# A planned matmul order: one 512-column matmul behind each narrow one, and new engine costs in the plan

## The chip, the core and the metric

The kernel runs on one core of one Trainium2 chip. The metric is the device time of one execution in microseconds; lower is better. A core has five engines with a queue of instructions each: TensorE (PE in the profile, with its weight loads as PEld), VectorE (DVE), ScalarE (ACT), GpSimd (POOL) and SyncE (SP). An engine takes its own instructions in order, and semaphores hold one engine for another. TensorE multiplies a stationary operand (the weights, loaded by LDWEIGHTS) with a moving one whose columns stream through, and writes to PSUM.

## What is computed

One layer of a trunk with 512 tokens and a width of 2048, in float32. A normalised input is projected to three branches (q, k, v and a gate, four heads of 128 each), to forget-gate logits and to three merge gates:

```python
hn = rmsnorm(x, norm_g)
proj = jnp.einsum('bsd,dc->bsc', hn, w_in)
...
gates = jax.nn.sigmoid(proj[..., QKVG_COLS + N_HEADS:] + b_gate).reshape(b, s, N_BRANCH, D_MODEL)
...
ya = forgetting_attention(qa, ka, to_heads(br[:, :, 0, 2]), f_logit)      # softmax with a decay bias
yb = chunked_relpos_attention(qb, kb, to_heads(br[:, :, 1, 2]), rel_bias)  # chunks with a relative bias
yc = stick_breaking_attention(...)                                         # causal, in log space
ys = ys * jax.nn.silu(br[:, :, :, 3])
up = jnp.einsum('bsnw,nwd->bsnd', ys, w_up)
merged = jnp.sum(gates * up, axis=2)
return x + jnp.einsum('bsd,de->bse', merged, w_out)
```

## The kernel before

**Products in parts.** A float32 matrix product is made of three single-pass products: each operand is split into a rounded high part (fp32r) and the rest, and high x high, low x high and high x low are added up in PSUM. The moving operand of the big products is a weight tile and always 512 columns wide, the stationary one a 128 x 128 block of the activations (`mm`, L264, whose instruction is L265). ScalarE makes the high part of a weight tile (`prep`, L366) and VectorE the low part (L371); two or three tiles are prepared ahead. Most of the input projection and the whole output projection go by a seven-product (Strassen) scheme, whose combinations of weights are added by a DMA that accumulates (`add_up`, issued by GpSimd at L281) and by VectorE (L574).

**Small work of the heads.** Twelve heads (four for each of the branches C, B, A) are handled beside the big products. For each head q, k and the gate are turned by TensorE, four 128-column transposes each (`turned`, L796, instruction L801). Scores are made by `mm3` (L258, instructions L260 to L262): for the query block i three matmuls of 128 x (i + 1) columns, so 128, 256, 384 and 512, with a further 128-column one for the mask in branch A (L898). The softmax or stick-breaking weights are turned again by `soft_trans` (L916, instruction L926; 4, 3, 2 and 1 transposes), and multiplied with the values by `av` (L1002, instructions L1014 to L1016; 512, 384, 256 and 128 columns). Later the merged outputs are turned by `turned_m` (L1275, instruction L1282), 64 transposes in four runs of 16, and `merged_b` (L1308) makes from them the parts that the output projection needs.

**What sets the order.** The order on TensorE, VectorE and ScalarE is fixed when the program is built, by a planner (`Flow`, L65) that imitates the three engines. Every piece of work is a Python generator that yields what it needs: an event, a number of buffers, or an engine with a cost. `run` (L125) takes, again and again, the offered step that can start first by the planned clocks, and among equal ones that with the earliest due time (its ready time plus the `slack` of its task); then it advances that engine's planned clock by the cost and issues the instructions. The main stream of big products (`stream`, L1412) is a task with a slack of 1e9, so that it gives way to all others and fills what they leave. Most tasks of the heads have 5, those of the last head 0.3 (its gate, values and SiLU 4). The costs come from three functions (L151 to L160):

```python
def mm_us(n, x=1):
    return x * max(0.115, n / 2400 + 0.0133)
def act_us(n, x=1):
    return x * (0.075 + 0.00095 * n)
def dve_us(n, x=1):
    return x * (0.1 + 0.00105 * n)
```

A group of narrow matmuls is one step: four transposes are offered as one step of 0.11 x 4, the three matmuls of `mm3` and `av` as one each. The transfers are imitated as well: `fetch` (L276, a load by SyncE) and `add_up` move on a planned line of transfers, `line`, and return an event with a landing time. These times decide only where an instruction is put in its queue; on the chip the semaphores decide when it starts.

Of the kernel before, what the change touches and what calls it, by code (L numbers as in the profile page):

```python
# [64 lines left out]
class Flow:  # L65
# [7 lines left out]
    def __init__(self):  # L73
        self.clock = [0.0] * 3
        self.idle = [0.0] * 3
        self.now = self.fin = 0.0
        self.tasks = []

    def set(self, event):
        event.t = self.fin  # L80
# [4 lines left out]
    def spawn(self, gen, slack, ready=None):  # L85
        task = Task(gen, slack, self.now if ready is None else ready)
        self.tasks.append(task)
        self.advance(task)

    def advance(self, task):  # L90
# [34 lines left out]
    def run(self):  # L125
        while self.tasks:
            best = None
            for t in list(self.tasks):
                if t.engine is None:
                    self.advance(t)  # L130
            for t in self.tasks:
                if t.engine is not None:
                    key = (max(self.clock[t.engine], t.ready), t.due)
                    if best is None or key < best[0]:
                        best = key, t
            assert best is not None, [
                (t.gen.__qualname__.split(".")[-1], t.gen.gi_frame.f_lineno,
                 (len(t.wait[0].free), t.wait[1]) if isinstance(t.wait, tuple) else "event") for t in self.tasks]
            (start, _), t = best
            e = t.engine  # L140
            self.idle[e] += start - self.clock[e]
            self.now = start
            self.clock[e] = start + t.cost
            t.ready = self.clock[e]
            self.fin = t.fin = self.clock[e] + self.LATE[e]
            t.prev = e
            t.engine = t.wait = None
            self.advance(t)


def mm_us(n, x=1):  # L151
    return x * max(0.115, n / 2400 + 0.0133)


def act_us(n, x=1):
    return x * (0.075 + 0.00095 * n)


def dve_us(n, x=1):
    return x * (0.1 + 0.00105 * n)  # L160


@with_exitstack
def hybrid_kernel(
# [50 lines left out]
    def blk(i):  # L215
        return slice(i * P, (i + 1) * P)
# [38 lines left out]

        nc.vector.scalar_tensor_tensor(to, a, -1.0, b, op0=ALU.mult, op1=ALU.subtract)

    def mm3(ps, lh, ll, rh, rl, start, stop, more=False):  # L258

        nc.tensor.matmul(ps, lh, rh, start=start, stop=False, skip_group_check=more)  # L260
        nc.tensor.matmul(ps, lh, rl, start=False, stop=False, skip_group_check=more)  # L261
        nc.tensor.matmul(ps, ll, rh, start=False, stop=stop, skip_group_check=more)  # L262

    def mm(ps, w, x, start=False, stop=False, more=False):  # L264
        nc.tensor.matmul(ps, w, x, start=start, stop=stop, skip_group_check=more)  # L265
# [13 lines left out]

    def add_up(to, src, ready, kb):  # L280
        nc.gpsimd.dma_start(to, src, accum_op=ALU.add)  # L281
        line[1] = max(line[1], ready + 1.0) + kb / 170.0
        return Event(line[1] + 2.5)

    def stored(slots, n, kb):

# [88 lines left out]
    def products(u, ps, kts, tbs, block, first=False, last=False, bank=None, done=None, outer=False):  # L375

        for group in [[tb] for tb in tbs] if outer else [tbs]:
            if bank is not None:
                for tb in group:
                    yield bank[0], 1  # L380
                    ps[tb] = bank[1]()
            for j, kt in enumerate(kts):
                for tb in group:
                    yield lambda: block(kt, tb) is not None
                    h, lo, ev = block(kt, tb)
                    yield ev
                    yield PE, mm_us(S, 2)
                    mm(ps[tb], h, u.hi[:, j, :], first and j == 0)
                    mm(ps[tb], lo, u.hi[:, j, :])
            yield u.ready  # L390
            for j, kt in enumerate(kts):
                for tb in group:
                    yield PE, mm_us(S)
                    mm(ps[tb], block(kt, tb)[0], u.lo[:, j, :], stop=last and j == len(kts) - 1)
            if last:
                for tb in group:
                    spawn(done(tb), 1.0, flow.fin)
# [347 lines left out]
    class Head:  # L745
# [49 lines left out]

        def turned(self, r):  # L796

            yield PE, 0.11 * QB
            ps = att()
            for tb in range(QB):  # L800
                nc.tensor.transpose(ps[:, blk(tb)], self.c[tb][:, blk(r)], identf)  # L801
            self.taken()
            return ps
# [81 lines left out]
        def soft_scores(self, i):  # L885
            n = self.n
            m = (i + 1) * P
            for e in (("p", Q), ("p", K), ("b",)):
                yield self.event(*e)
            yield atts, 1  # L890
            (qh, ql), (kh, kl) = self.t[Q], self.t[K]
            yield PE, mm_us(m, 3) + (mm_us(P) if n == A else 0)
            ps = att()[:, :m]
            mm3(ps, qh[:, blk(i)], ql[:, blk(i)], kh[:, :m], kl[:, :m], True, n == B)
            p = self.p[i]
            mx, sm = small("mx"), small("sm")
            if n == A:
                nc.tensor.matmul(ps[:, blk(i)], identb, mska, start=False, stop=True)  # L898
# [12 lines left out]
            nc.vector.reciprocal(sm, sm)  # L911
            yield ACT, act_us(m) + 0.1
            nc.scalar.activation(p, p, AF.Copy, scale=sm)
            set_(self.event("s", i))

        def soft_trans(self, j):  # L916
            for i in range(QB):
                yield self.event("s", i)
            if j:
                yield self.event("a", j - 1)  # L920
            yield from self.parts_of(j)
            yield atts, 1
            yield PE, 0.11 * (QB - j)
            ps = att()
            for i in range(j, QB):
                nc.tensor.transpose(ps[:, blk(i)], self.p[i][:, blk(j)], identf)  # L926
# [16 lines left out]
        def stick_scores(self, i):  # L943
# [5 lines left out]
            yield PE, mm_us(m, 3)  # L949
            ps = att()[:, :m]  # L950
            mm3(ps, qh[:, blk(i)], ql[:, blk(i)], kh[:, :m], kl[:, :m], True, True)
            if self.nth("s", QB):
                give(t2s, 4)
            z = self.p[i]
# [47 lines left out]
        def av(self, j):  # L1002
# [3 lines left out]
                yield self.event("o", j - 1)  # L1006
            else:
                yield atts, 1
            yield PE, mm_us(S - j * P, 3)
# [4 lines left out]
            nc.tensor.matmul(o, vh[:, blk(j)], h, start=j == 0, stop=False)  # L1014
            nc.tensor.matmul(o, vl[:, blk(j)], h, start=False, stop=False)  # L1015
            nc.tensor.matmul(o, vh[:, blk(j)], lo, start=False, stop=j == QB - 1)  # L1016
            set_(self.event("o", j))
            give(t2s, (2, 0, 2, 4)[j])
# [58 lines left out]
    def quad(parts, g, done, early=False):  # L1077
# [8 lines left out]
        def mms(kts):  # L1086
            def go(u):
# [9 lines left out]
                else:  # L1097
# [3 lines left out]
                    for part in range(3):  # L1101
                        if part == 2:
                            yield u.ready
                        for j, kt in enumerate(kts):
                            yield (raw_hi[kt], raw_ev[kt], raw_ev[kt])[part]
                            yield PE, mm_us(S, QB)
                            w = u.lo if part == 2 else u.hi
                            for tb in tbs:
                                mm(ps[tb], block(kt, tb)[part == 1], w[:, j, :], kt + part == 0)
                if early and (kts[-1] + 1) % 4 == 0:  # L1110
                    four = range(kts[-1] - 3, kts[-1] + 1)
# [91 lines left out]
    def split_y(i):  # L1203
        def go():
# [3 lines left out]
            if (n, h) == (A, NH - 1):  # L1208
                yield last_head.event("y")
                t = last_head.y  # L1210
            else:
                yield t2s, 1
                t = t2("yr")
                yield fetch(t, yd[n, h], flow.now, 256)
# [60 lines left out]
    def turned_m(g, i):  # L1275
        for tb in range(QB):
            yield merged_ev[NB - 1, g, tb]
        yield atts, 1
        yield PE, 0.11 * QB
        ps = att()  # L1280
        for tb in range(QB):
            nc.tensor.transpose(ps[:, blk(tb)], merged[g, tb][:, blk(i)], identf)  # L1282
        turns[g] = turns.get(g, 0) + 1
        if turns[g] == QB:
# [207 lines left out]
```

## Time and profile before

| | before |
|---|---|
| median of 3 runs | 1319.29 us (1318.65 to 1319.43) |
| the profiled execution | 1319.42 us |
| its span, first to last instruction | 1317.7 us |
| TensorE busy, matmuls | 1307.4 us, 6034 |
| VectorE busy | 1023.4 us (78%) |
| ScalarE busy | 752.4 us (57%) |
| GpSimd busy | 91.5 us (7%) |
| moved by DMA | 266.03 MB |
| granted TensorE clock | 1.00 |

A row of the timeline gives the start in us from the span's start, the duration, the engine, the line, the operation, the tiles (out<-in), the shape and how many instructions were merged into the row; in brackets stands idle time ahead of it with what ended it. A row of a group has the count after the x, then the busy time and the mean duration in ns, then idle time of the engine just ahead of the group. Matmuls overlap: the next one starts while the last is still draining, so the share of busy time and the mean duration don't say what one costs; the distance from start to start does. In a row of waits stand the engine and line that waited, what released it, the total in us, the number of times and the longest.

### The profile page before, as it was taken

To read this page: it belongs to the slowest core of one execution; us is meant where nothing else is said; L and a number is where in the kernel's file an instruction comes from. 1 tells how busy PE (TensorE), PEld (TensorE's weight loads), DVE (VectorE), ACT (ScalarE), POOL (GpSimd) and SP (SyncE) were. 2 spreads that over 40 slices of the span, in tenths; PEclk is the share of its full clock that TensorE was granted. 3 is DMA by queue.
4 is the path that set the end of the run, shared out by engine and by line. 5 is a ranking of instruction groups with operands and counts; after the bars stand their busy time and mean duration, and the time that the engine had idled before them with its cause. 6 is when DMAs were issued, how large, how long until landed. Compare 5 with 4: busy or idle time off the path is not lost.

```text
span 1317.7 us, 17190 instructions
## 1 busy us (share of the span) xinstructions
PE 1307.4 (99%) x6034; PEld 1078.6 (82%) x6034; DVE 1023.4 (78%) x1420; ACT 752.4 (57%) x1271; POOL 91.5 (7%) x115
## 2 busy tenths in 40 slices
PE   9999999999999999999999999999999999999998
PEld 7788888888888888888888888888887788878787
DVE  6877787887878777687776877778789668798667
ACT  7655464564557646566466664667558545454342
POOL 0000001110011101111011110111000000000110
PEclk9999999999999999999999999999999999999999
DMA  9745677866777757777577775777786656637883
GB/s 361 233 121 145 181 210 191 235 170 180 211 192 229 201 164 232 175 228 203 170 225 176 225 207 168 224 177 217 225 250 196 236 192 205 164 95 250 246 240 128
DMA packets 89063, 266.03 MB, mean 202 GB/s; under 512 B 11264, under 2 KB 11264, under 8 KB 88976
## 3 DMA queue, kind: packets, MB, share of 16 engines
q1 hardware_dynamic: 71552, 206.16, 46.1%
q0 software_dynamic: 14976, 54.53, 23.2%
q10 hardware_dynamic: 2448, 4.24, 0.8%
q8 instruction: 47, 0.77, 0.2%
q14 instruction: 40, 0.33, 0.1%
HBM read 245.19 MB, written 19.70 MB: 201 GB/s over the span
## 4 chain that ended last, share of the span: by engine, by line
PE 95%; DMA 2%; ACT 1%; DVE 1%; issue 0%; POOL 0%; ACTq 0%; POOLq 0%; DVEq 0%
PE acc L265 87%; DMA raw<-in_w_out 2%; PE att L801 1%; PE att L926 1%; PE att L260 1%; PE att L261 1%; PE att L262 1%; DMA raw<-in_w_col 1%; PE att L1016 1%; PE att L1015 1%; PE att L1282 1%; ACT wh L366 1%; PE att L265 1%; PE att L1014 0%; DMA sg<-gl 0%; DVE wl L371 0%
## 5 line engine op out<-in xcount | busy, mean ns | idle before, releaser
L371 DVE TENSOR_TENSOR wl<-raw,wh 128x1024 fp32r<-128x1024 f32 (+1 forms) x405 | 493.4, 1220 | 209.5 <-PE acc L265 122.7
L366 ACT ACTIVATE wh<-raw 128x1024 fp32r<-128x1024 f32 (+1 forms) x405 | 426.7, 1055 | 369.5 <-PE acc L265 283.2
L265 PE MATMUL acc<-wh,x 128*128 128x512 f32 x1664 | 429.5, 392 | 0.0
L265 PEld LDWEIGHTS acc<-wh,x 128*128 128x128 f32 x1664 | 308.8, 188 | 65.7 <-ACT xn L476 1.7
L265 PE MATMUL acc<-wh,t 128*128 128x512 f32 x1056 | 272.7, 391 | 0.0
L265 PE MATMUL acc<-wl,x 128*128 128x512 f32 x832 | 230.1, 390 | 0.0
L265 PEld LDWEIGHTS acc<-wh,t 128*128 128x128 f32 x1056 | 196.7, 188 | 40.3
L265 PEld LDWEIGHTS acc<-wl,x 128*128 128x128 f32 x832 | 155.8, 188 | 33.0 <-DVE wl L371 0.4
L265 PE MATMUL acc<-wl,t 128*128 128x512 f32 x528 | 149.3, 390 | 0.0
L281 POOL DMA_DIRECT2D raw<-in_w_col x88 | 76.3, 867 | 878.1 <-DMA raw<-in_w_col 198.2
L574 DVE TENSOR_TENSOR raw<-raw,raw 128x1024 f32<-128x1024 f32 x104 | 126.7, 1218 | 0.0
L265 PEld LDWEIGHTS acc<-wl,t 128*128 128x128 f32 x528 | 98.4, 188 | 19.6
L265 PE MATMUL acc<-wh,m 128*128 128x512 f32 x416 | 105.2, 390 | 1.5 <-ACT wh L366 1.4
L265 PE MATMUL acc<-wh,y 128*128 128x512 f32 x384 | 103.7, 390 | 1.3 <-DVE sg L1248 1.3
L265 PEld LDWEIGHTS acc<-wh,m 128*128 128x128 f32 x416 | 77.9, 188 | 18.5 <-ACT wh L366 2.3
L265 PEld LDWEIGHTS acc<-wh,y 128*128 128x128 f32 x384 | 71.7, 188 | 16.8 <-DVE sg L1248 2.2
L265 PE MATMUL acc<-wl,y 128*128 128x512 f32 x192 | 59.7, 391 | 0.0
L265 PE MATMUL acc<-wl,m 128*128 128x512 f32 x208 | 58.1, 390 | 0.1
L246 ACT ACTIVATE ah<-att 128x512 fp32r<-128x512 f32 (+3 forms) x48 | 21.0, 438 | 48.1 <-PE att L926 48.1
L265 PEld LDWEIGHTS acc<-wl,m 128*128 128x128 f32 x208 | 38.9, 188 | 8.5 <-DVE wl L371 0.5
L250 DVE TENSOR_TENSOR al<-att,ah 128x512 fp32r<-128x512 f32 (+3 forms) x48 | 23.5, 490 | 25.5 <-ACT ah L246 24.8
L265 PEld LDWEIGHTS acc<-wl,y 128*128 128x128 f32 x192 | 35.7, 188 | 7.3
(179 smaller groups left out, 1115.9 us busy)
## 6 DMA issues: line engine op xcount, KB each, us to landing
raw<-in_w_col SPq DMA_DIRECT2D x235, 512.0 KB, 5.0
raw<-in_w_col POOLq DMA_DIRECT2D x88, 512.0 KB, 8.0
raw<-in_w_out SPq DMA_DIRECT2D x40, 512.0 KB, 3.6
raw<-in_w_up SPq DMA_DIRECT2D x24, 512.0 KB, 3.6
sg<-gl SPq DMA_DIRECT2D x48, 256.0 KB, 5.0
raw<-in_w_out POOLq DMA_DIRECT2D x16, 512.0 KB, 5.9
gl<-u SPq DMA_DIRECT2D x22, 256.0 KB, 9.2
gl<-s SPq DMA_DIRECT2D x22, 256.0 KB, 4.6
```

The costliest lines, as they stand in the source:

```text
L246: nc.scalar.activation(hi, src, AF.Copy)
L250: nc.vector.tensor_sub(lo, src, f(hi))
L260: nc.tensor.matmul(ps, lh, rh, start=start, stop=False, skip_group_check=more)
L261: nc.tensor.matmul(ps, lh, rl, start=False, stop=False, skip_group_check=more)
L262: nc.tensor.matmul(ps, ll, rh, start=False, stop=stop, skip_group_check=more)
L265: nc.tensor.matmul(ps, w, x, start=start, stop=stop, skip_group_check=more)
L281: nc.gpsimd.dma_start(to, src, accum_op=ALU.add)
L366: nc.scalar.activation(u.hi, u.raw, AF.Copy)
L371: nc.vector.tensor_sub(u.lo, u.raw, f(u.hi))
L574: nc.vector.tensor_add(to.raw, to.raw, self.raw)
L801: nc.tensor.transpose(ps[:, blk(tb)], self.c[tb][:, blk(r)], identf)
L926: nc.tensor.transpose(ps[:, blk(i)], self.p[i][:, blk(j)], identf)
```

## The change

Four things are changed.

1. `run` remembers whether TensorE's last step was a narrow one (a cost under 0.2, so up to 384 columns) of another task than the main stream. If so, and if the main stream offers a matmul that is ready at that time, all other TensorE steps are passed over, except those of tasks with a slack below 1.
2. The groups of matmuls are offered one at a time: the transposes (a cost of `TURN` each), `mm3`, `av`, and the pairs and fours in the main stream.
3. The costs: no lower bound of 0.115 for a matmul, 0.05 for a transpose, and higher fixed parts for VectorE and ScalarE. The planned landing of an accumulating transfer is the later of its source's landing and the line's time, plus 6.5, and the line is advanced less.
4. `split_y`, which loads a stored branch output again, first waits in the plan for the event that it was written.

```diff
+        self.main = None
+        self.narrow = False
...
+        if slack > 1e8:
+            self.main = task
...
+            main = self.main
+            full = (self.narrow and main is not None and main.engine == PE
+                    and main.ready <= self.clock[PE] + 0.02)
             for t in self.tasks:
+                if full and t.engine == PE and t is not main and t.slack >= 1:
+                    continue
...
+            if e == PE:
+                self.narrow = t is not self.main and t.cost < 0.2
...
-def mm_us(n, x=1):
-    return x * max(0.115, n / 2400 + 0.0133)
+def mm_us(n):
+    return n / 2400 + 0.0133
+
+
+TURN = 0.05
...
-    return x * (0.075 + 0.00095 * n)
+    return x * (0.13 + 0.0009 * n)
...
-    return x * (0.1 + 0.00105 * n)
+    return x * (0.15 + 0.00105 * n)
...
-        nc.tensor.matmul(ps, lh, rh, start=start, stop=False, skip_group_check=more)
-        nc.tensor.matmul(ps, lh, rl, start=False, stop=False, skip_group_check=more)
-        nc.tensor.matmul(ps, ll, rh, start=False, stop=stop, skip_group_check=more)
+        nc.tensor.matmul(ps, lh, rh, start=start, stop=False)
+        yield PE, mm_us(m)
+        nc.tensor.matmul(ps, lh, rl, start=False, stop=False)
+        yield PE, mm_us(m)
+        nc.tensor.matmul(ps, ll, rh, start=False, stop=stop)
...
-        line[1] = max(line[1], ready + 1.0) + kb / 170.0
-        return Event(line[1] + 2.5)
+        line[1] += kb / 250.0
+        return Event(max(line[1], ready) + 6.5)
...
-            yield PE, 0.11 * QB
+            yield PE, TURN
             ps = att()
             for tb in range(QB):
+                if tb:
+                    yield PE, TURN
                 nc.tensor.transpose(ps[:, blk(tb)], self.c[tb][:, blk(r)], identf)
...
             else:
+                yield heads[i].event("y")
                 yield t2s, 1
```

`soft_trans` and `turned_m` are changed as `turned` is; `av` yields ahead of each of its three matmuls, and the main stream ahead of each of its own. No matmul is added or taken away.

More of the change, by code (lines that the diff above doesn't have):

```diff
@@ L256, in minus, with mm3 @@
         nc.vector.scalar_tensor_tensor(to, a, -1.0, b, op0=ALU.mult, op1=ALU.subtract)
[L258 to L262, printed above, removed]
+    def mm3(ps, lh, ll, rh, rl, start, stop, m):
+        nc.tensor.matmul(ps, lh, rh, start=start, stop=False)
[3 more added lines that the diff above has]
+        nc.tensor.matmul(ps, ll, rh, start=False, stop=stop)
     def mm(ps, w, x, start=False, stop=False, more=False):
@@ L386, in products @@
                     yield ev
-                    yield PE, mm_us(S, 2)
+                    yield PE, mm_us(S)
                     mm(ps[tb], h, u.hi[:, j, :], first and j == 0)
+                    yield PE, mm_us(S)
                     mm(ps[tb], lo, u.hi[:, j, :])
@@ L891, in soft_scores @@
             (qh, ql), (kh, kl) = self.t[Q], self.t[K]
-            yield PE, mm_us(m, 3) + (mm_us(P) if n == A else 0)
+            yield PE, mm_us(m)
             ps = att()[:, :m]
-            mm3(ps, qh[:, blk(i)], ql[:, blk(i)], kh[:, :m], kl[:, :m], True, n == B)
+            yield from mm3(ps, qh[:, blk(i)], ql[:, blk(i)], kh[:, :m], kl[:, :m], True, n == B, m)
             p = self.p[i]
@@ L897, in soft_scores @@
             if n == A:
+                yield PE, mm_us(P)
                 nc.tensor.matmul(ps[:, blk(i)], identb, mska, start=False, stop=True)
@@ L922, in soft_trans @@
             yield atts, 1
-            yield PE, 0.11 * (QB - j)
+            yield PE, TURN
             ps = att()
             for i in range(j, QB):
+                if i > j:
+                    yield PE, TURN
                 nc.tensor.transpose(ps[:, blk(i)], self.p[i][:, blk(j)], identf)
@@ L948, in stick_scores @@
             (qh, ql), (kh, kl) = self.t[Q], self.t[K]
-            yield PE, mm_us(m, 3)
+            yield PE, mm_us(m)
             ps = att()[:, :m]
-            mm3(ps, qh[:, blk(i)], ql[:, blk(i)], kh[:, :m], kl[:, :m], True, True)
+            yield from mm3(ps, qh[:, blk(i)], ql[:, blk(i)], kh[:, :m], kl[:, :m], True, True, m)
             if self.nth("s", QB):
@@ L1008, in av @@
                 yield atts, 1
-            yield PE, mm_us(S - j * P, 3)
+            n = mm_us(S - j * P)
+            yield PE, n
             if j == 0:
@@ L1014, in av @@
             nc.tensor.matmul(o, vh[:, blk(j)], h, start=j == 0, stop=False)
+            yield PE, n
             nc.tensor.matmul(o, vl[:, blk(j)], h, start=False, stop=False)
+            yield PE, n
             nc.tensor.matmul(o, vh[:, blk(j)], lo, start=False, stop=j == QB - 1)
@@ L1105, in go @@
                             yield (raw_hi[kt], raw_ev[kt], raw_ev[kt])[part]
-                            yield PE, mm_us(S, QB)
                             w = u.lo if part == 2 else u.hi
                             for tb in tbs:
+                                yield PE, mm_us(S)
                                 mm(ps[tb], block(kt, tb)[part == 1], w[:, j, :], kt + part == 0)
@@ L1278, in turned_m @@
         yield atts, 1
-        yield PE, 0.11 * QB
+        yield PE, TURN
         ps = att()
         for tb in range(QB):
+            if tb:
+                yield PE, TURN
             nc.tensor.transpose(ps[:, blk(tb)], merged[g, tb][:, blk(i)], identf)
```

## The prediction

> **What bounds the kernel now.** I began with the page: the span, the busy shares and the chain that ended last.
>
> ```profile
> span 1317.7 us, 17190 instructions
> PE 1307.4 (99%) x6034; PEld 1078.6 (82%) x6034; DVE 1023.4 (78%) x1420; ACT 752.4 (57%) x1271; POOL 91.5 (7%) x115
> PE 95%; DMA 2%; ACT 1%; DVE 1%; issue 0%; POOL 0%; ACTq 0%; POOLq 0%; DVEq 0%
> ```
>
> TensorE is busy for 99% of the span and is 95% of the chain. A better order on VectorE or ScalarE can therefore gain only what TensorE still waits for. The view of waits, for TensorE alone, shows how much that is:
>
> ```profile
> PE att L417 <- DVE identb L310: 1.9, 1, 1.9
> PE acc L265 <- ACT wh L366: 1.4, 1, 1.4
> PE acc L265 <- DVE sg L1248: 1.3, 1, 1.3
> PE att L265 <- DVE wl L371: 1.1, 1, 1.1
> PE att L801 <- ACT w L793: 0.4, 1, 0.4
> ```
>
> The first wait is the start-up, ahead of the planned order. The other four, 1.4 + 1.3 + 1.1 + 0.4 = 4.2 us, are all that a better order could win, 0.3% of the span. Everything else is the sum of what TensorE's instructions cost in the place where they stand, so the question is what a narrow matmul costs behind a narrow one and what it costs between two wide ones. The mean durations of the groups don't say this, because matmuls overlap. The distance from start to start in the timeline does. First the wide ones, undisturbed:
>
> ```profile
> 1294.51 1.98 PE L265 MATMUL acc<-wh,m 128*128 128x512 f32 x8
> 1296.33 1.07 PE L265 MATMUL acc<-wl,m 128*128 128x512 f32 x4
> 1297.23 1.98 PE L265 MATMUL acc<-wh,m 128*128 128x512 f32 x8
> ```
>
> Twelve matmuls start in 1297.23 - 1294.51 = 2.72 us, which is 0.227 us each.
>
> **A narrow matmul among narrow ones.** Sixteen transposes in a row, with wide ones around them:
>
> ```profile
> 1053.54 1.08 PE L265 MATMUL acc<-wh,y 128*128 128x512 f32 x4
> 1054.46 1.91 PE L1282 MATMUL att<-identf,sg 128*128 128x128 f32 x16
> 1056.12 0.70 PE L265 MATMUL acc<-wl,y 128*128 128x512 f32 x2
> 1056.66 1.09 PE L265 MATMUL acc<-wh,y 128*128 128x512 f32 x4
> ```
>
> From 1053.54 to 1056.66 are 3.12 us. Six wide matmuls take 6 x 0.227 = 1.36, and 1.76 are left for sixteen transposes: 0.110 us each.
>
> **A narrow matmul between wider ones.** The order of before has one kind of place where a transpose stands alone, the last of each head's `soft_trans`. A wide matmul is ahead of it and a 256-column one behind:
>
> ```profile
> 217.86 1.08 PE L265 MATMUL acc<-wh,t 128*128 128x512 f32 x4
> 218.78 0.27 PE L926 MATMUL att<-identf,p 128*128 128x128 f32 x1
> 218.81 0.36 PE L1014 MATMUL att<-ah,vh 128*128 128x256 f32 x1
> 219.01 0.28 PE L1015 MATMUL att<-ah,vl 128*128 128x256 f32 x1
> 219.13 0.28 PE L1016 MATMUL att<-al,vh 128*128 128x256 f32 x1
> 219.25 0.63 PE L265 MATMUL acc<-wl,t 128*128 128x512 f32 x2
> ```
>
> From 217.86 to 219.25 are 1.39 us. Four wide ones take 0.91. The 256-column ones take 0.12 each (219.01 to 219.13 to 219.25), so three take 0.36. That leaves 0.12 us for the lone transpose. It is not cheaper than in a run. The start shown behind it comes 0.03 us later, but the next one comes 0.20 later where 0.12 is usual: the matmul behind it has begun and stands. I read this as its weights not being there. A load fits under a wide matmul, but the load of the matmul *behind* a narrow one has only the narrow one to lie under.
>
> The same with 128-column score matmuls (`mm3`):
>
> ```profile
> 171.44 1.07 PE L265 MATMUL acc<-wh,x 128*128 128x512 f32 x4
> 172.34 0.22 PE L260 MATMUL att<-qkh,qkh 128*128 128x128 f32 x1
> 172.40 0.28 PE L261 MATMUL att<-qkl,qkh 128*128 128x128 f32 x1
> 172.51 0.27 PE L262 MATMUL att<-qkh,qkl 128*128 128x128 f32 x1
> 172.63 1.13 PE L265 MATMUL acc<-wh,x 128*128 128x512 f32 x4
> 173.60 1.07 PE L265 MATMUL acc<-wl,x 128*128 128x512 f32 x4
> ```
>
> From 171.44 to 173.60 are 2.16 us. Eight wide ones take 1.81, three narrow ones 0.35, or 0.115 each. After the first, whose weights came in under a wide matmul, only 0.06 passes (172.34 to 172.40): that is the streaming of 128 columns. The shortfall comes back at the end, where four wide ones take 173.60 - 172.63 = 0.97 and not 0.91. So each matmul costs the longer of two times, its own streaming (0.227, 0.12, 0.06) and the load behind it (about 0.11). Such a sum doesn't depend on the order.
>
> The Trainium skill, TensorE: Matmul & The Clock Gate, section LDWEIGHTS (loading the stationary operand), gives a load as its columns over 1.2 GHz, by estimate 107 ns for 128 columns, whatever stands ahead; this speaks against the change, and the rows agree. The same page, section Back-to-back issue gap, has an isolated 128-column matmul at 128/2.4 + 2.5, by estimate 56 ns; where that governed, a narrow one between wide ones would cost half of what the lone transpose above shows.
>
> **The change, part by part.** *The rule in `run`.* After a narrow matmul that isn't the main stream's, the next one must be the main stream's if that is ready, except for tasks of slack below 1 (the last head's scores, transposes and `qk`). `turned`, `soft_trans`, `turned_m`, `mm3` and `av` now offer their matmuls one by one, so that the rule reaches them. The transposes:
>
> ```profile
> L926 PE MATMUL att<-identf,p 128*128 128x128 f32 x120 | 20.8, 271 | 0.0
> L801 PE MATMUL att<-identf,v 128*128 128x128 f32 x66 | 12.8, 274 | 0.0
> L801 PE MATMUL att<-identf,w 128*128 128x128 f32 x66 | 12.8, 273 | 0.4 <-ACT w L793 0.4
> L1282 PE MATMUL att<-identf,sg 128*128 128x128 f32 x64 | 7.6, 272 | 0.0
> L801 PE MATMUL att<-identf,c 128*128 128x128 f32 x12 | 1.8, 272 | 0.0
> ```
>
> They are 328: 22 for each of twelve heads (three turns of 4, and 4 + 3 + 2 + 1) and 64 in `turned_m`. The places where one follows another directly are 15 in a head and 60 in the four runs of 16, 240 in all. The last head keeps 12 of its 15, which leaves 228 to be split. What one split costs is the difference between the lone transpose and one in a run, 0.12 - 0.11 = 0.01 us, with both ends read from rows of two decimals: between 0 and 0.02. The sum is 228 x 0.01 = +2.3 us, with bounds of 0 and +4.6. I take the middle, since the rows themselves stand there. A split below zero is excluded by the lone one's 0.12, unless a 512-column matmul behind differs from a 256-column one; that is the first rival.
>
> The 128-column scores and `av` products cost 0.115 in a run, and the sum of longer times gives the same when each has a wide one behind it: 0. The 256- and 384-column ones stream for longer (0.12 and more) than a load takes and hide it already: 0.
>
> *The transposes come later.* A run of four is now spread over three more wide matmuls, 3 x 0.227 = 0.7 us, and sixteen over fifteen, 3.4 us. TensorE does main work meanwhile; what comes later is ScalarE's and VectorE's work on the result. Costed at nothing: attention keeps a whole head of distance from its consumer, and ScalarE prepares weights well ahead:
>
> ```profile
> ACT wh L366 <- PE acc L265: 283.2, 178, 5.7
> ```
>
> In 178 places ScalarE had already waited for TensorE to release a weight buffer, 283.2/178 = 1.6 us on average. That is the cover; a jam longer than this reaches TensorE.
>
> *The costs.* VectorE's and ScalarE's become more exact: for 1024 columns the plan had 0.1 + 0.00105 x 1024 = 1.175 us and now has 1.225, and for 512 on ScalarE it had 0.561 and now has 0.591.
>
> ```profile
> L371 DVE TENSOR_TENSOR wl<-raw,wh 128x1024 fp32r<-128x1024 f32 (+1 forms) x405 | 493.4, 1220 | 209.5 <-PE acc L265 122.7
> L643 ACT ACTIVATE u<-acc 128x512 f32<-128x512 f32 x26 | 15.5, 597 | 11.4 <-PE acc L265 11.3
> ```
>
> Measured are 1.220 and 0.597. TensorE's become less exact: a transpose is planned at 0.05 (it was 0.11), a 128-column matmul at 0.067 (it was 0.115), so in a head the plan runs ahead of TensorE by about 22 x 0.06 = 1.3 us. No queue is re-ordered by hand; the queues of VectorE and ScalarE follow the plan, and a queue that has an early consumer of a TensorE result holds up the weight conversions behind it. Together I put both at -0.5 us, one of the smaller waits gone, with ends of -4.2 (all of them gone) and about +4 (their like again).
>
> *`add_up`.* The accumulating transfer now lands in the plan at its source's landing or the queue's time, whichever is later, plus 6.5 us:
>
> ```profile
> raw<-in_w_col POOLq DMA_DIRECT2D x88, 512.0 KB, 8.0
> ```
>
> Measured is 8.0. Before, with the queue free, it was also 1.0 + 512/170 + 2.5 = 6.5, but it pushed back every later transfer in the plan. Which transfer is issued when hangs on freed buffers, so nothing moves on the queues of SyncE and GpSimd but by the plan's new times. Zero, with the ends in the previous item. The wait for a stored branch output in `split_y` is long fulfilled by then: zero.
>
> **Sum.** The profiled execution took 1319.42 us, beside a median of 1319.29. With +2.3 - 0.5 = +1.8 it would be 1321.2, and against the median 1321.1; I say 1321.1, which is 0.14% up. About 0.2% (2.6 us) is what a measurement of this kernel can tell from no change, so the forecast is "the same, on the slow side".
>
> **Rivals.** *A narrow matmul between 512-column ones costs its streaming alone, 0.06.* It would need the load of the wide one's weights to start before the narrow one does. About 310 transposes would gain 0.05 and some 66 score and output products 0.055: 15.5 + 3.6 = 19 us, so 1300. Against it stand the lone transpose and the last `mm3` product above, both already with something wider behind. By the 56 ns of the Trainium skill (TensorE: Matmul & The Clock Gate, section Back-to-back issue gap) the 310 transposes alone would gain an estimated 17 us. Chance 0.05.
>
> *The waits go.* With true costs most of the 4.2 us fall away and the splits cost nearly nothing: about 1319.3 - 3.5 = 1316. For it: all four are waits for VectorE or ScalarE. Against it: the wait for `wh` (1.4) is behind a weight transfer, which no cost mends. Chance 0.15.
>
> *Slower: late transposes jam VectorE ahead of the weights.* The place is the start of the output projection, where the last sixteen transposes feed `merged_b`, whose VectorE and ScalarE work stands in one queue with the weight splits of L371.
>
> ```profile
> 1157.51 1.91 PE L1282 MATMUL att<-identf,sg 128*128 128x128 f32 x16
> 1186.12 5.44 PE att L265 x24
> ```
>
> The first row is the timeline's, the second the chain's, where the matmuls that use these parts begin. In between TensorE waits 1.1 us for L371 as it is. If the splits of the merged parts come 3.4 us later, L371 waits behind more of them, and the wait grows towards 1.1 + 3.4; with the splits' 2.3 the kernel is at about 1325. It decides if the cover at L371 there is under those 3.4 us, which a wait of 1.1 suggests; against it, 27 us lie between the transposes and their use, and the plan sees the lateness. Together with the upper half of the splits' bounds: chance 0.33.
>
> *The rule changes little*, since main isn't ready in the plan when it asks: then 1319. This is inside "same".
>
> **How the numbers follow.** The forecast's case (same) has 0.47, slower 0.33, faster 0.15 + 0.05 = 0.20. The range goes from 1316, the centre of the waits' rival, to 1325, the jam's time: about 0.12 is left below and 0.07 above. "Same" alone would be 1316.7 to 1321.9.
>
> **What would show it.** The transposes' groups should keep their counts, and in the timeline each should stand alone between L265 rows. From wide to wide across one the distance should be 0.227 + 0.12. If it is 0.28, the first rival holds. The four waits of TensorE, in particular that for L371 near 1174 us, tell the other two apart. The prediction is wrong if TensorE's waits change by more than 2 us or if a lone transpose costs under 0.10 or over 0.14 us.

## The result, and the profile after

The changed kernel takes 1324.21 us (median of 5 runs, 1324.16 to 1328.08) where the kernel before takes 1319.29: the ratio is 1.0044, 95% interval 1.003 to 1.0058. It is slower by about 5 us. "The same, on the slow side" was wrong; the time lies inside the range, near its upper end.

The page of the changed kernel, of an execution of 1328.08 us:

```profile
span 1326.4 us, 17218 instructions
PE 1313.2 (99%) x6034; PEld 1074.5 (81%) x6034; DVE 1018.5 (77%) x1420; ACT 751.5 (57%) x1271; POOL 91.5 (7%) x115
```

The matmul count is that of before, and VectorE and ScalarE do no more. TensorE is still busy for 99%. This execution is the longest of the five. TensorE's clock was down to half in places in it, which explains a part of that (seven matmuls at 0.2 us too much, 1.4 us) and which the experiments come back to; a second profile of the same kernel, of an execution of 1325.42 us, lies beside the experiments.

The transposes in the timeline, TensorE's rows near 953 us (lines are from the changed file: L281 is the big product, L948 `soft_trans`):

```profile
952.62 0.62 PE L281 MATMUL acc<-wh,x 128*128 128x512 f32 x2
953.07 0.39 PE L281 MATMUL acc<-wl,x 128*128 128x512 f32 x1
953.30 0.27 PE L948 MATMUL att<-identf,p 128*128 128x128 f32 x1
953.33 0.48 PE L281 MATMUL acc<-wl,x 128*128 128x512 f32 x1
953.65 0.27 PE L948 MATMUL att<-identf,p 128*128 128x128 f32 x1
953.68 0.49 PE L281 MATMUL acc<-wh,x 128*128 128x512 f32 x1
954.00 0.27 PE L948 MATMUL att<-identf,p 128*128 128x128 f32 x1
954.03 0.48 PE L281 MATMUL acc<-wh,x 128*128 128x512 f32 x1
954.35 0.27 PE L948 MATMUL att<-identf,p 128*128 128x128 f32 x1
954.38 0.71 PE L281 MATMUL acc<-wh,x 128*128 128x512 f32 x2
954.92 0.62 PE L281 MATMUL acc<-wl,x 128*128 128x512 f32 x2
```

The rule does what it says. From 952.62 to 954.92 are 2.30 us with eight wide matmuls (8 x 0.227 = 1.816) and four transposes, which leaves 0.484, or 0.121 us for each; over the twelve heads a lone transpose takes 0.117 on average. In a run of sixteen they took 0.110. A 512-column matmul behind a narrow one hides nothing: its start is shown 0.03 us after the transpose's, and then it takes 0.32 until the next one starts.

TensorE's waits after:

```profile
PE acc L281 <- DVE sg L1274: 4.4, 3, 2.3
PE att L434 <- DVE identb L326: 1.9, 1, 1.9
PE acc L281 <- ACT wh L382: 1.7, 2, 1.4
PE att L281 <- DVE wl L387: 0.3, 1, 0.3
PE att L281 <- ACT wh L382: 0.3, 1, 0.3
PE acc L281 <- DVE wl L387: 0.2, 1, 0.2
PE att L1041 <- DVE al L264: 0.2, 1, 0.2
```

Without the start-up they were 4.2 us and are 7.1. The wait for the merge gates (`sg`) has grown from 1.3 to 4.4, and the one for the low parts at the output projection has shrunk from 1.1 to 0.3. The first of these is at the end of the last head. ScalarE's row and TensorE's rows there:

```profile
1030.08 1.28 ACT L1258 ACT_TABLE_LOAD   x1
1032.79 1.19 PE L281 MATMUL acc<-wh,y 128*128 128x512 f32 x4 [1.58 <-DVE sg L1274]
1038.08 1.50 PE L281 MATMUL acc<-wh,y 128*128 128x512 f32 x4 [2.26 <-DVE sg L1274]
1039.37 1.05 PE L281 MATMUL acc<-wl,y 128*128 128x512 f32 x2
1040.22 1.91 PE L281 MATMUL acc<-wh,y 128*128 128x512 f32 x4
```

The sigmoids of the merge gates come after the last head's last exponential, with a table load ahead of them (1030.08). They let the up projection's banks go, so TensorE stops until they are through. Before, the table load stood here:

```profile
1024.66 1.28 ACT L1232 ACT_TABLE_LOAD   x1
```

Counted in the traces, the main stream had by then started 4113 wide matmuls; in the changed kernel it had started 4128 and had no bank left. So the last head ends later not only by the clock but against the main work. And behind the second wait, two matmuls take 1040.22 - 1039.37 = 0.85 us, 0.43 each and not 0.227.

### The profile page after: what moved, and what is told of

The parts are those of the page before. It is cut to its first block, busy times and chain, and to the rows that moved or that the text cites. A ratio compares the mean times of both kernels' runs of the same rounds, so it can differ in the third digit from the quotient of the medians.

```text
span 1326.4 us, 17218 instructions
## 1 busy us (share of the span) xinstructions
PE 1313.2 (99%) x6034; PEld 1074.5 (81%) x6034; DVE 1018.5 (77%) x1420; ACT 751.5 (57%) x1271; POOL 91.5 (7%) x115
## 4 chain that ended last, share of the span: by engine, by line
PE 96%; DMA 1%; DVE 1%; ACT 1%; issue 0%; POOL 0%; DVEq 0%; ACTq 0%; SPq 0%; POOLq 0%
PE acc L281 89%; PE att L820 1%; PE att L948 1%; DMA raw<-in_w_out 1%; DMA xr<-in_xn 1%; PE att L281 1%; PE att L276 1%; PE att L278 1%; PE att L1310 1%; PE att L274 1%; PE att L1039 1%; PE att L1041 1%; PE att L1037 0%; ACT sg L1258 0%; DVE wl L387 0%; PE att L434 0%
## 5 line engine op out<-in xcount | busy, mean ns | idle before, releaser
L281 PE MATMUL acc<-wh,x 128*128 128x512 f32 x1664 | 448.6, 400 | 0.0
L281 PEld LDWEIGHTS acc<-wh,x 128*128 128x128 f32 x1664 | 309.7, 188 | 71.9 <-ACT small_n L479 0.9
L281 PE MATMUL acc<-wh,t 128*128 128x512 f32 x1056 | 284.8, 396 | 0.0
L281 PE MATMUL acc<-wl,x 128*128 128x512 f32 x832 | 236.8, 395 | 0.0
L281 PEld LDWEIGHTS acc<-wh,t 128*128 128x128 f32 x1056 | 196.6, 188 | 43.7
L281 PEld LDWEIGHTS acc<-wl,x 128*128 128x128 f32 x832 | 155.8, 188 | 34.4
L281 PE MATMUL acc<-wl,t 128*128 128x512 f32 x528 | 151.8, 394 | 0.0
L281 PEld LDWEIGHTS acc<-wl,t 128*128 128x128 f32 x528 | 99.1, 188 | 21.9
L281 PE MATMUL acc<-wh,y 128*128 128x512 f32 x384 | 107.8, 401 | 4.4 <-DVE sg L1274 4.4
L281 PE MATMUL acc<-wh,m 128*128 128x512 f32 x416 | 106.3, 392 | 1.7 <-ACT wh L382 1.7
L281 PEld LDWEIGHTS acc<-wh,m 128*128 128x128 f32 x416 | 77.9, 188 | 19.0 <-ACT wh L382 2.5
L281 PEld LDWEIGHTS acc<-wh,y 128*128 128x128 f32 x384 | 72.3, 189 | 21.3 <-DVE sg L1274 5.3
L281 PE MATMUL acc<-wl,y 128*128 128x512 f32 x192 | 61.7, 401 | 0.0
L281 PE MATMUL acc<-wl,m 128*128 128x512 f32 x208 | 58.6, 393 | 0.3 <-DVE wl L387 0.2
L281 PEld LDWEIGHTS acc<-wl,m 128*128 128x128 f32 x208 | 38.9, 188 | 9.4 <-DVE wl L387 1.2
L281 PEld LDWEIGHTS acc<-wl,y 128*128 128x128 f32 x192 | 36.5, 191 | 8.3
```

## The experiments

The theory (S) to begin with: the splits cost about 2 us, and the other 3 are the late end of the last head, which comes from the new plan. Its rivals: the splits are free and all is waiting (W), or it is the spreading that makes the last head late (R). Ratios are to the kernel before, timed beside each. The last two columns cut the span of each profiled execution in two: from the last group of forget-gate products (L1141; L1116 before) to the first turn of the last head, that of its gate, and from there to the end. Up to that turn all kernels do the same work, 3819 wide matmuls of the main stream (3820 where groups are one step) and as many narrow ones of each width, counted in the traces.

| kernel | median us | ratio, 95% interval | to the gate's turn, us | from there on, us |
|---|---|---|---|---|
| before | 1319.29 | 1 | 940.3 | 323.8 |
| changed, the first time | 1324.21 | 1.0044 (1.003 to 1.0058) | 942.5 | 329.5 |
| changed, rule off | 1324.10 | 1.0037 (1.0024 to 1.0049) | 939.5 | 328.4 |
| before, with rule and one-by-one offers (and the event in `split_y`) | 1325.62 | 1.0048 (1.0035 to 1.006) | 942.3 | 328.9 |
| changed, old costs of VectorE and ScalarE | 1324.61 | 1.0038 (1.0026 to 1.0051) | 942.6 | 326.8 |
| before, with the new landing alone | 1318.29 | 0.9988 (0.9979 to 0.9997) | 941.1 | 322.9 |
| changed, once more | 1325.89 | 1.0050 (1.0038 to 1.0062) | 942.5 | 327.8 |
| changed, five buffers kept | 1322.74 | 1.0023 (1.0014 to 1.0033) | 942.5 | 325.5 |
| the same, rule off | 1319.90 | 1.0009 (1.0000 to 1.0017) | 939.5 | 325.4 |
| before, new landing, four buffers kept | 1315.91 | 0.9974 (0.9964 to 0.9984) | 940.6 | 319.7 |
| five buffers kept, idle stretch filled | 1322.08 | 1.0019 (1.001 to 1.0028) | 942.5 | 323.8 |
| five buffers kept, last scores grouped | 1322.85 | 1.0025 (1.0016 to 1.0034) | 942.5 | 323.6 |
| landing, four buffers, new costs of VectorE, ScalarE | 1316.67 | 0.9983 (0.9974 to 0.9991) | 940.5 | 320.2 |
| landing, four buffers, rule and one-by-one offers | 1319.54 | 0.9999 (0.999 to 1.0008) | 942.6 | 321.8 |

The first stretch is the same within 0.3 us in all kernels with the rule, and in both without it but with single offers: there the rule shows without waits. The second has the waits and the slow clock in it, and varies.

**One part undone or done alone.** The first four. The rule off:

```diff
-            full = (self.narrow and main is not None and main.engine == PE
+            full = (False and self.narrow and main is not None and main.engine == PE
```

> The changed kernel with the rule switched off: no task is passed over for the main stream, all else as changed (matmuls offered one by one, new costs, new landing of accumulating transfers). Theory S (the loss of 4.9 us has two parts: 234 transposes moved out of their runs, at 118 ns each where one in a run takes 110, so about 1.9 us with some tenths for the score products; and about 3 us of waiting around the end of the last head, which comes from the plan's costs): transposes stand in runs of four again, and the time is 2 to 2.5 us under the changed kernel, about 1322, with the waits for the merge gates after the last head unchanged. Rival W (the splits cost nothing, all of the loss is waiting): within 0.7 us of the changed kernel, 1324. Rival R (spreading is what makes the last head late, so the waits go with the rule): about 1319.

It came out at 1324.1, which alone would speak for W. But its profile has other waits: 3.8 us for the merge gates, and 1.6 for low parts of weights (0.9 + 0.7), where the changed kernel has 0.3 + 0.2. So two things moved at once, and the median decides nothing about the rule. The trace does: to the gate's turn this kernel takes 2.9 us less than the changed one, which speaks against W, and loses it again behind (328.4 us, where the changed kernel's second profile has 327.8). R falls too, since the waits for the gates stay without the spreading.

The changed kernel with every cost and the landing put back, which leaves the rule, the one-by-one offers and the event in `split_y`:

```diff
-TURN = 0.05
+TURN = 0.11
-    return n / 2400 + 0.0133
+    return max(0.115, n / 2400 + 0.0133)
```

(and the three other costs likewise)

> The kernel before with the rule and the one-by-one matmuls alone; all costs (TensorE's, VectorE's, ScalarE's) and the landing of accumulating transfers as before. Theory S: about 2 us over the kernel before, 1321.3, with TensorE's waits near the 4.2 us of before. Rival W: 1319.3. Rival R: about 1324, with TensorE's waits around the end of the last head as in the changed kernel.

1325.6, over what theory S allows. In its profile the wait for the merge gates is 2.6 us in one piece. It shows that the late last head needs neither the new costs nor the new landing.

> The changed kernel with the old, lower costs of VectorE and ScalarE; rule, matmul costs and landing as changed. Theory S with the higher costs as the origin of the late last head: the waits for the merge gates shrink by about 2 us and the time is about 1322. If the origin is another one (the matmul costs or the landing), the time stays at about 1324.

1324.6: no gain in time, though the wait for the gates is 1.7 us in its profile; the higher costs of VectorE and ScalarE aren't the origin.

```diff
-        line[1] = max(line[1], ready + 1.0) + kb / 170.0
-        return Event(line[1] + 2.5)
+        line[1] += kb / 250.0
+        return Event(max(line[1], ready) + 6.5)
```

> The kernel before with the new landing of accumulating transfers alone. The landing decides only where conversions stand in the queues. If it is the origin of the late last head, the time is about 1322; if the higher engine costs are, it stays within 1 us of before, 1318.5 to 1320.

1318.3, ratio 0.9988: the landing is a small gain by itself. Its profile, of the longest of its eleven executions, doesn't show where.

**What makes the last head late.** In the changed kernel's trace the last head's second operand is turned 26 wide matmuls after the first, in the kernel before 14. Between the two it needs two of the 20 shared 128x512 buffers (`qk`), and the theory (B) is that it stands waiting for them in the plan, since tasks with more slack hold them. The variant leaves five buffers to the last head, from the start of its small work until its last parts exist:

```diff
+    def keep(k):
+        def go():
+            t2s.kept = k
+            return
+            yield
+        return go
+
+    at(end - 2 * CH - 0, keep(5))
...
         yield last_head.event("hl", 2)
+        t2s.kept = KEPT
```

> The changed kernel, word for word, beside its variants on one chip, for a second profile. The first one showed TensorE at half its clock for 7 matmuls (426 ns from start to start) right after two waits of 1.9 and 2.7 us near 1035 us. Theory S (splits about 2 us, the rest is the end of the last head: late scores, waits for the merge gates, and the clock dip that these waits set off): 1324, with the same milestones of the last head and the dip again if both waits are there. If the dip was an accident of that execution, the waits come without it.

> The changed kernel with five of the 20 shared 128x512 buffers left to the last head from the time its small work begins until its last parts exist (before: one). Theory B (the last head is late because its second operand waits for two of these buffers, which tasks with more slack have taken): the second turn follows the first within some 15 wide matmuls where 26 lay between them, the waits for the merge gates shrink from about 4 us to under 2, no clock dip there, and the time is 1320 to 1321, with the splits' 2 us left. Rival D (the work on VectorE and ScalarE between scores and turned weights makes it late): the turns move but the waits stay, 1323 to 1324.

The turns of the last head's two operands in TensorE's timeline, L801 of the kernel before first, then L820 of the changed kernel's second profile, then the variant's:

```profile
997.58 0.62 PE L801 MATMUL att<-identf,w 128*128 128x128 f32 x2 [0.36 <-ACT w L793]
...
1001.84 0.38 PE L801 MATMUL att<-identf,w 128*128 128x128 f32 x2
```

```profile
1002.06 0.38 PE L820 MATMUL att<-identf,w 128*128 128x128 f32 x2
...
1008.48 0.38 PE L820 MATMUL att<-identf,w 128*128 128x128 f32 x2
```

```profile
1002.86 0.38 PE L820 MATMUL att<-identf,w 128*128 128x128 f32 x2
...
1004.23 0.38 PE L820 MATMUL att<-identf,w 128*128 128x128 f32 x2
```

The second turn follows after 4.3, 6.4 and 1.4 us. The waits for the gates, in the changed kernel's second profile and in the variant's:

```profile
PE acc L281 <- DVE sg L1274: 2.7, 3, 1.6
PE acc L281 <- DVE sg L1284: 2.6, 2, 2.1
```

Both have the half clock behind them. The time falls from 1325.89 to 1322.74, 3.2 us, in the middle between theory B's 1320 to 1321 and D's 1323 to 1324. So the buffers are shown to be a cause, but not by the way that B names: the wait for the gates is as long as in the second profile without them. In the two profiles 2.4 us of the gain stand behind the gate's turn (327.8 against 325.5). 0.9 of them are in the waits (5.8 against 4.9 us without the start-up), partly those for high parts of weights. Another part is short delays inside the last head's own products, which are too short for the view of waits: its three 256-column `av` matmuls take 0.91 us in the changed kernel (1028.82 to 1029.73) and 0.35 in the variant (1029.34 to 1029.69). Nor does a late second turn cost time by itself: with the new landing alone it follows after 7.7 us (1000.36 to 1008.10), in a kernel that is faster than before.

**The rule by itself**, with the last head mended in both kernels:

> As the kernel with five buffers kept, and the rule off as well. With the end of the last head mended in both, the difference between the two is the price of the rule alone. Theory S: 2 to 2.5 us faster than with the rule, about 1318.5. Rival W (splits are free): the same time.

1319.90 against 1322.74: the rule costs 2.8 us. The profiles say where. The stretch up to the turn of the last head's gate, in which both do the same work, with the rule and without:

```profile
54.22 1.04 PE L1141 MATMUL att<-x,small_in 128*4 128x512 f32 x8
...
996.68 0.27 PE L820 MATMUL att<-identf,w 128*128 128x128 f32 x1
```

```profile
53.26 1.04 PE L1141 MATMUL att<-x,small_in 128*4 128x512 f32 x8
...
992.79 0.38 PE L820 MATMUL att<-identf,w 128*128 128x128 f32 x2
```

942.46 us with the rule, 939.53 without: 2.93 more, and the changed kernel with and without it shows the same two times. From wide to wide in these traces, a lone transpose takes 0.117 us on average and one in a run of four 0.110. Lone score and product matmuls of 128, 256 and 384 columns take 0.117, 0.124 and 0.184, and in runs of three 0.112, 0.120 and 0.179. For 242 transposes and 202 of the others that makes, by estimate, 1.6 + 0.9 us; the rest isn't separated.

**Filling the idle stretch.** In the variant with five buffers one long wait for the gates, of 2.1 us, is left, and TensorE is slow behind it:

```profile
1032.25 1.19 PE L281 MATMUL acc<-wh,y 128*128 128x512 f32 x4 [2.12 <-DVE sg L1284]
1033.28 0.87 PE L281 MATMUL acc<-wl,y 128*128 128x512 f32 x2
1033.95 1.91 PE L281 MATMUL acc<-wh,y 128*128 128x512 f32 x4
1035.66 1.05 PE L281 MATMUL acc<-wl,y 128*128 128x512 f32 x2
1036.51 1.27 PE L281 MATMUL acc<-wh,y 128*128 128x512 f32 x4
```

Six matmuls from 1033.95 to 1036.51 take 2.56 us, 0.427 each, almost twice 0.227. The stretches of the same profile give the granted clock, in the column after the engines' busy times:

```profile
1030.00:1040.00 10.00, 7.88 (x29) 6.24 (x28) 4.28 (x8) 7.48 (x13) 0.00 (x0) 0.83 1.04 391
```

0.83 of full speed over these 10 us. The variant puts nine extra matmuls into a spare bank there (their result is used by nobody):

```diff
+                if (g, b, i) == FILL:
+                    yield last_head.event("o", QB - 1)
+                    yield atts, 1
+                    spare = att()
+                    for j in range(NFILL):
+                        yield PE, mm_us(S)
+                        nc.tensor.matmul(spare, u.hi[:, 0, :P], u.hi[:, j % 2, :], start=True, stop=True)
+                    give(atts)
...
+FILL, NFILL = (0, 1, 0), 9
```

> The kernel with five buffers kept, and nine extra 512-column matmuls (into a spare bank, read by nobody) in TensorE's queue just behind the last head's last value product, ahead of the matmul that waits 2.2 us for the merge gates there. Their 9 x 0.227 = 2.0 us lie inside that wait. Theory C (the eight matmuls at 426 ns after the wait are TensorE's clock, which is taken down by the idle time itself): no step of 426 ns there, granted clock 1.0, and about 1.5 us less, 1321.2, although TensorE does more work. Rival (the slow matmuls come from the work on the other engines at that moment, or by chance): the eight stay, 1322.7 or a little more.

```profile
1030.00 2.28 PE L1307 MATMUL att<-wh 128*128 128x512 f32 x9
1032.28 1.19 PE L281 MATMUL acc<-wh,y 128*128 128x512 f32 x4
1033.32 0.62 PE L281 MATMUL acc<-wl,y 128*128 128x512 f32 x2
1033.78 1.07 PE L281 MATMUL acc<-wh,y 128*128 128x512 f32 x4
```

No slow step: two matmuls in 0.46 us behind it. The median fell by 0.7 to 1322.08 and not by 1.5, with overlapping intervals and on another chip. The next kernel shows why: the clock doesn't fall each time.

**Scores in one step.** In the last head alone, three matmuls of a score block are one step again:

```diff
-            yield PE, mm_us(m)
+            yield PE, mm_us(m) * (3 if self.last else 1)
```

(with the two yields inside `mm3` left out there)

> The kernel with five buffers kept, with the three matmuls of a score block offered as one step again in the last head alone. In the changed kernels the four score blocks of the last head go in turns, so that all end together 1.7 us after the start, where in the kernel before the first block is done after 0.3 us. Theory G (this is why the turned weights come 37 wide matmuls after the scores, and 28 before): the distance falls by about 5 and the wait for the merge gates by about 1 us, to 1321.5. Rival (VectorE or ScalarE is busy with other work then, so the first block wouldn't start earlier): unchanged, 1322.7.

Unchanged, 1322.85. The first of the turned weights come 37 wide matmuls after the first scores, as without it: theory G falls. But its profile, of an execution of 1321.52 us, has the same wait and no slow matmul behind it:

```profile
1031.76 1.19 PE L283 MATMUL acc<-wh,y 128*128 128x512 f32 x4 [2.12 <-DVE sg L1286]
1032.79 0.62 PE L283 MATMUL acc<-wl,y 128*128 128x512 f32 x2
1033.24 1.07 PE L283 MATMUL acc<-wh,y 128*128 128x512 f32 x4
```

So a wait of 2.1 us is followed by the half clock in some executions only. Of this kernel's eleven executions the three with a granted clock of 0.998 took 1323.6 to 1324.7 us and the six with 1.000 took 1321.5 to 1322.9; with the stretch filled, on the same chip, nine of eleven have 1.000. That the clock falls because of the wait is likely, since the slow steps stood only behind waits and at the start, and weren't there in the one profile with the wait filled; it isn't shown. Two executions of the kernel with four buffers and new costs have 0.998 as well, though its profile has no wait for the gates.

**A faster version, and the parts on top of it.** The kernel before with the new landing and four buffers kept for the last head, then the new costs of VectorE and ScalarE on top of that, and the rule with the one-by-one offers on top of it (old costs):

> The kernel before with the new landing of accumulating transfers and four buffers kept for the last head; old costs, groups of narrow matmuls as before, no rule. If theories S and B hold, this leaves out what costs and keeps what helps: about 1316 to 1317, faster than both kernels. If the buffers don't matter, 1318.3 as with the landing alone.

> The fast variant (kernel before, new landing, four buffers kept) with the new costs of VectorE and ScalarE and nothing else. The plan with these costs has the last head later by some 5 us of waiting. If the higher costs do harm by themselves, 1318 to 1320; if they only describe the engines better, 1316 or less.

> The fast variant (new landing, four buffers kept, old costs of all engines) with the rule and the one-by-one matmuls. Theory S: the splits cost 2.8 us as they did between the two kernels with five buffers, so 1318.7, in the stretch of the twelve heads 0.13 us more in each 41 us slice. Rival W: 1316.

The first takes 1315.91 us, faster than both kernels, ratio 0.9974. TensorE's waits in it:

```profile
PE att L417 <- DVE identb L310: 1.9, 1, 1.9
PE att L265 <- DVE wl L371: 1.1, 1, 1.1
PE acc L265 <- ACT wh L366: 0.9, 1, 0.9
```

The wait for the merge gates is gone. The new costs on top give 1316.67, ratio 0.9983: the intervals overlap, so no help and no great harm is shown; the result lies between its two expectations. The rule and the one-by-one offers on top of the first give 1319.54, 2.9 over the kernel with the new costs and 3.6 over the first, which was timed on another chip. Its expectation of 1318.7 and W's 1316 lie below. Here there is no wait for the gates in the profile, and of the loss 2.0 us stand before the gate's turn and 2.1 behind it.

## Why the prediction was wrong

*The split of the runs* was right. Predicted were 2.3 us (0 to 4.6), from the lone transpose that the kernel before already had. Against the kernel before, the stretch up to the last head's gate takes 2.4 us more (942.46 - 940.33, and 0.23 for one wide matmul less); against single offers without the rule it is 2.8 in the medians and 2.93 in the traces. That the size fits so well is partly luck: a split costs 0.007 us rather than 0.01, and the score and product matmuls, put at 0, cost about 0.005 each. The rival by which a narrow matmul would cost 0.06 fell: it costs 0.12.

*The step that failed* is the pair of small terms, "costed at nothing: attention keeps a whole head of distance from its consumer" and the -0.5 us for costs and order. The distance is there for eleven heads. The last head's consumer is the up projection right behind it, and what it holds up are the merge gates. There the wait grew from 1.3 to 4.4 us, 2.7 in the second profile, where I took the waits to shrink. From the turn of the last head's gate to the end the kernel before takes 323.8 us and the changed one 329.5 and 327.8 in its two profiles, half clock included. In the medians, 4.9 us less the 2.1 of the first stretch leave about 2.8 for what comes behind; some 0.4 of it are, by estimate, the 60 splits of the late transposes (0.007 each). So this term was about +2.4 instead of -0.5, and leaving five buffers to the last head took 3.2 us back. The working had the row of this wait (`sg`, 1.3 us) and counted it only as something to win. The prediction's own sign of being wrong, waits that change by more than 2 us, came true in the first profile (4.2 to 7.1).

*Why any new order makes it late*: the first three kernels with single offers, with old or new costs, with the rule or without, all had waits for the gates of 1.7 us or more. The new landing alone has 1.8 as well, and a late second turn. That the order of before gets its two buffers in time looks like luck; this is argued, not shown. The new costs of VectorE and ScalarE are cleared by two runs, as far as the medians tell. The new TensorE costs (0.05 for a transpose) were not tried alone, and the longer way from scores to turned weights (37 wide matmuls instead of 28) isn't explained: both stay open, though the fastest kernel has 34 and no wait for the gates. With rule off and five buffers kept, 1319.90 is still above the landing alone, 1318.29 on another chip, and carries a wait of 2.1 us for the gates.

*The landing* was put at zero and gains about 1.3 us (0.9988).

*The slower rival* had the right sign and a mechanism of the right kind, late small work ahead of what TensorE needs, but the wrong place: the wait for the low parts near the output projection fell from 1.1 to 0.3 us.

*The clock* stood in no step. A slow stretch of eight matmuls costs 8 x 0.2 = 1.6 us, in some executions. In both profiles of the changed kernel there is one, of seven matmuls.

## What to carry to other kernels

A matmul with 128 columns cost 0.110 us in a run here and 0.117 between wide ones, not the 0.06 of its streaming; look for one that already stands alone in the trace before paying for an order that isolates them. When a static plan is made anew, look first at the task that ends a phase and at the shared buffers that it must get: priority in time doesn't help a task that finds no buffer. A waiting engine's small rows can grow as well as shrink under a new plan, and the longest of them is where to look.

## What the runs showed of the hardware

TensorE ran at half speed behind waits that are short: 0.427 us for a 512-column matmul, for seven or eight matmuls, so 3.0 to 3.4 us, after waits of 1.6 (the changed kernel's second profile) to 2.6 us (the kernel before with the rule and one-by-one offers). The waits of 1.58 us in the changed kernel's first profile, of 1.62 in the variant with landing, four buffers and rule, and of 2.12 in the one with grouped scores were without effect, and so were those of up to 1.4 us in the kernel before. The Trainium skill, TensorE: Matmul & The Clock Gate, section What's actually happening, has the clock go to half after a window of about 3.4 us of idle time that runs freely and doesn't start anew with a kernel. The length of the slow stretch, 8 x 0.427 = 3.4 us, agrees with such a window, and that the same wait has an effect only sometimes agrees with its running freely; but no wait here was as long as 3.4 us, and the measurement decides: less can be enough.
